# Splits of mixer B and of the memory queued behind the gates' evictions in a fused decoder layer

## The chip, the cores and the metric

The kernel runs on one core of a Trainium2 chip. The five engines of a core are named as the profile names them, and each has a queue of instructions of its own: TensorE (PE: matmuls), VectorE (DVE), ScalarE (ACT), GpSimd (POOL) and SyncE (SP, which issues the DMA transfers here). The metric is the device time of one execution in microseconds (us); the median of several executions is given.

## The reference

One layer of a decoder over 256 tokens of width 1024, in float32. Its core, with the helper functions left out:

```python
h = rmsnorm(x, norm_w[l])
proj = h @ w_in[l]                       # q, k, v of three dilation groups (mixer A), of mixer B, gates, ...
o_a = dilated_mixture(groups, slopes_a)  # 3 groups, 8 heads of 64, ALiBi, causal windows
o_b = moba_attention(heads(b_q), heads(b_k), heads(b_v), slopes_b)   # 8 heads, one block of 256 here
kv = rmsnorm(mem, mem_norm_w[l]) @ w_mem_kv[l]
o_m = memory_cross_attention(heads(m_q), heads(m_k), heads(m_v))     # 4 heads, 256 memory tokens
p_a = (o_a * jax.nn.silu(a_gate)) @ w_branch_a[l]
p_b = (o_b * jax.nn.silu(b_gate)) @ w_branch_b[l]
p_m = (o_m * jax.nn.silu(m_gate)) @ w_branch_m[l]
g_a, g_b, g_m = jnp.split(jax.nn.sigmoid(merge_logits + b_merge[l]), N_BRANCHES, axis=-1)
x = x + (g_a * p_a + g_b * p_b + g_m * p_m) @ w_out[l]
return rmsnorm(x, final_norm_w)
```

## The kernel before

All weights are cut into chunks of 128 x 2048 numbers (1 MB) that a list, PLAN, puts in order. Chunks 0 to 5 make mixer B's queries, keys and values (Bq, Bk, Bv), 6 and 7 the gate of mixer B, 8 and 9 the gate of mixer A, 10 the gate of the memory branch, 11 its query (Mq), 12 and 13 its keys and values (Mk, Mv), 14 and on mixer A, then the merge gates, the branch projections and the output projection. The loop over PLAN does for chunk i: start the load of chunk i + 3 on SP, split chunk i + 2, multiply, evict.

Splitting means that a float32 number is kept as two numbers of the type fp32r, which the matmuls take: ACT casts (`wh`, L93), DVE subtracts that from the number and keeps what is left (`wl`, L94). Each projection is then three matmuls per 128 rows: high by high and low by high (L232, L233, alternating), and at the end of a half chunk eight of high by low weights (L235). A chunk has two halves of 24 matmuls. There are three buffers for raw weights, three for `wh`, two for `wl`, so a load waits for the split of the chunk three before, and the split of the lower part of a chunk for PE's end of the chunk two before.

Outputs of a chunk lie in one of three PSUM banks (pool `pj`), so chunk i + 3 can begin only when chunk i is evicted. A gate is evicted by a tanh on ACT (`thg`, L645) and one instruction on DVE (`g`, L647) that reads the bank a second time.

Mixer B's queries and keys are split too, per half of the heads: `split_q` (two instructions on ACT, L271, two on DVE, L272) and `split_k` (four and four, L283 and L284, L289 and L290). The memory is scaled and split by eight instructions on ACT (`mh`, L218) and eight on DVE (`ml`, L219), and its mean squares by two on ACT (L171). In the loop these stand at chunks 6 to 11, in the middle of the projections that don't need them yet: the first to read Bq, Bk and the memory's parts is chunk 12.

The attention of mixer B runs in four pairs of heads (`pair_steps_b`): scores on PE (`sb`), a reduction and an exponential, a normalisation on DVE (`u`, L313 and L314), six transposes on PE (`pt`, L320), a copy on ACT, the product with the values (`ob`). Its steps are put into the loop at half chunks by a list of due times (`chain` and `pump`): the first pair's scores stand in the middle of chunk 12, its transposes in the middle of chunk 13, the second pair's transposes in chunk 14.

PE's order is that of the program from chunk 8 on. On the other engines a scheduler orders the instructions by its own estimate of when each is ready, unless `tc.issue_after` says that one is to stand behind another on its queue.

Of the kernel before, what the change touches and what calls it, by code (L numbers as in the profile page):

```python
# [1 line left out]

# [8 lines left out]
AF = mybir.ActivationFunctionType  # L11
ALU = mybir.AluOpType
# [51 lines left out]
def kernel(ctx: ExitStack, tc: tile.TileContext, wts: bass.AP, xT_d: bass.AP, memT_d: bass.AP,  # L64
                      x_d: bass.AP, mem_d: bass.AP, xr_d: bass.AP, fnw_d: bass.AP, con_d: bass.AP, out: bass.AP):
    nc = tc.nc
# [85 lines left out]
    for k in range(KD):  # L152
        nc.scalar.activation(xh[:, k, :], xT[:, k, :], AF.Copy, scale=nw[:, k:k + 1])
        nc.vector.scalar_tensor_tensor(xl[:, k, :], xT[:, k, :], nw[:, k:k + 1], xh[:, k, :].bitcast(F32),
                                       op0=ALU.mult, op1=ALU.subtract)
# [53 lines left out]
    def mem_norm():  # L209
        memst["r"], memst["dg"] = stats(memst["nat"], "m")  # L210
# [54 lines left out]
    def split_q(src, scale, name):  # L265

        xs = []
        for s in range(2):
            own, other = halves(s)
            t = rp.tile([P, 512], F32R, tag="r", name=f"{name}x{s}")  # L270
            nc.scalar.mul(t[own], src[own], scale)  # L271
            nc.vector.scalar_tensor_tensor(t[other], src[own], scale, t[own].bitcast(F32), op0=ALU.mult,  # L272
                                           op1=ALU.subtract)
            xs.append(t)
        return [t.rearrange("p (f t) -> p f t", f=2) for t in xs]

    def split_k(src, name):

        ys, zs = [], []
        for s in range(2):  # L280
            own, other = halves(s)
            t = rp.tile([P, 512], F32R, tag="r", name=f"{name}y{s}")
            nc.scalar.copy(t[own], src[own])  # L283
            nc.scalar.copy(t[other], src[own])  # L284
            ys.append(t)
        for s in range(2):
            own, other = halves(s)
            z = rp.tile([P, 512], F32R, tag="r", name=f"{name}z{s}")
            nc.vector.tensor_tensor(z[own], src[own], ys[s][own].bitcast(F32), op=ALU.subtract)  # L289
            nc.vector.tensor_tensor(z[other], src[own], ys[s][own].bitcast(F32), op=ALU.subtract)  # L290
            zs.append(z)
        return [t.rearrange("p (f t) -> p f t", f=2) for t in ys + zs]
# [6 lines left out]
    qkv, gate, og, steps, ths, acc = {}, {}, {}, [], {}, {}  # L299
# [224 lines left out]
                cs = slice(512 * (n // 2), 512 * (n // 2 + 1))  # L524
                nc.sync.dma_start(out[P * t:P * (t + 1), cs], yt[:, cs])

    late = []

    def evac_b(i, kind, key, ps, ps1):
        t = qkv[kind, key] = rtile(f"{kind}{key}")  # L530
# [15 lines left out]
    for i, (kind, key, src, col) in enumerate(PLAN):  # L546
# [15 lines left out]
        if i + 2 < NCH:  # L562
            for j in range(2 if i < 2 else 1):
                split(i + 2, j, 4 if i < 2 else 2)
        if i in (6, 8):
            hf = (i - 6) // 2
            qkv["Bqx", hf] = split_q(qkv["Bq", hf], 1.0, f"Bq{hf}")
        if i in (7, 11):
            hf = (i - 7) // 4
            qkv["Bkx", hf] = split_k(qkv["Bk", hf], f"Bk{hf}")  # L570
        if i == 9:
            mem_norm()
        if i in (10, 11):
            mem_split(4 * (i - 10), 4 * (i - 9))
        nat = kind[0] == "B"
        ah, al = (XH, XL) if nat else (HH, HL)
        if src == "mem":
# [4 lines left out]
        else:  # L582
            if i == 0:
                pss = [pa.tile([P, 512], F32, tag=("s", "pt")[f // 2], name=f"pj0{f}") for f in range(4)]
            elif i > 1:
                ps = pj.tile([P, 512], F32, tag="pj", name=f"pj{i}")
# [17 lines left out]
        if kind[0] == "B":  # L604
            late.append((i, kind, key) + ((pss[2 * i], pss[2 * i + 1]) if i < 2 else (ps, None)))
            if i >= 3:
                for z in [z for z in late if i == 5 or z[0] > 1]:
                    evac_b(*z)
                    late.remove(z)
                if i > 3:  # L610
                    split_h(4 * i - 16, 4 * i - 12)
                if i < 5:

                    with tc.issue_after(lower[i + 1].ins):
                        make_h(4 * i - 12, 4 * i - 8)
        elif kind in ("Aq", "Ak", "Av", "Mq", "Mk", "Mv"):
            at = (kind,) + (key if kind[0] == "A" else (0,))
            if kind[1] == "q" and at[-1] == 0:
                qkv[at] = split_q(ps, -SCALE, f"{kind}{i}")
            elif kind == "Mk":  # L620
                t = rtile("Mk")
                nc.vector.tensor_tensor(t.rearrange("p (f t) -> p f t", f=2), ps.rearrange("p (f t) -> p f t", f=2),
                                        rb["m"][:, None, :].to_broadcast([P, 2, S]), op=ALU.mult)
                qkv[at] = split_k(t, f"{kind}{i}")
            elif kind == "Mv":
                t = qkv[at] = rtile(f"{kind}{i}")
                for n in range(2):
                    nc.scalar.activation(t[:, S * n:S * (n + 1)], ps[:, S * n:S * (n + 1)], AF.Copy,
                                         scale=memst["r"][:, n:n + 1])
            elif kind[1] == "k" and at[-1] == 0:  # L630
                qkv[at] = split_k(ps, f"{kind}{i}")
            elif kind == "Av" and key[1] > 0:

                hf, g = key
                if g == 1:
                    stacked[hf] = tp.tile([P, 2, 2, S], F32, tag="vs", name=f"vs{hf}")
                for r in range(2):
                    nc.scalar.copy(stacked[hf][64 * (g - 1):64 * g, :, r, :],
                                   ps[64 * r:64 * (r + 1)].rearrange("p (e c) -> p e c", e=2))
            else:  # L640
                t = qkv[at] = rtile(f"{kind}{i}")
                nc.scalar.mul(t, ps, -SCALE if kind == "Aq" else 1.0)
        elif kind == "G":
            th = tp.tile([P, 512], F32, tag="th", name="thg")
            nc.scalar.activation(th, ps, AF.Tanh, scale=0.5)  # L645
            g = gate[key] = rp.tile([P, 512], F32, tag="g", name=f"g{i}", bufs=5)
            nc.vector.scalar_tensor_tensor(g, th, 1.0, ps, op0=ALU.add, op1=ALU.mult)  # L647
        elif kind == "L":
            br, bk = key
            th = ths[br, bk] = tp.tile([P, 512], F32, tag="th", name="thl")  # L650
            off = {"a": 0, "b": 8, "m": 16}[br]
            for n in range(2):
                c = off + 2 * bk + n
                nc.scalar.activation(th[:, S * n:S * (n + 1)], ps[:, S * n:S * (n + 1)], AF.Tanh, bias=hb[:, c:c + 1],
                                     scale=0.5)
        elif kind == "W":
            br, hf = key
            kn = 2 if br == "m" else 4
            oh = [og[br, k][0] for k in range(kn)]
            ol = [og[br, k][1] for k in range(kn)]  # L660
            if "t" not in acc:
                acc["t"] = cp.tile([P, 4, 512], F32, tag="xt", name="acc")
            for j in range(2):
                bk = 2 * hf + j
                ps = pj.tile([P, 512], F32, tag="pj", name=f"pw{i}{j}")
                for n in range(2):
                    mm_feat(ps, S * n, i, kn, 512, 2 * j + n, oh, ol)
                    if j == 1 and n == 0 and i + 2 < NCH:
                        split(i + 2, 1, 2)
                a = acc["t"][:, bk, :]  # L670
                if br == "b":
                    nc.vector.scalar_tensor_tensor(a, ths[br, bk], 1.0, ps, op0=ALU.add, op1=ALU.mult)
                else:
                    tmp = tp.tile([P, 512], F32, tag="mt", name="mt", bufs=1)
                    nc.vector.scalar_tensor_tensor(tmp, ths[br, bk], 1.0, ps, op0=ALU.add, op1=ALU.mult)
                    if br == "m":
                        nc.gpsimd.tensor_tensor(a, a, tmp, op=ALU.add)
                    else:
                        nc.vector.tensor_tensor(a, a, tmp, op=ALU.add)
                        mh = rp.tile([P, 2, S], F32R, tag="r", name=f"mgh{bk}")  # L680
                        ml = rp.tile([P, 2, S], F32R, tag="r", name=f"mgl{bk}")
                        nc.scalar.copy(mh.rearrange("p a b -> p (a b)"), a)
                        nc.vector.tensor_tensor(ml.rearrange("p a b -> p (a b)"), a,
                                                mh.rearrange("p a b -> p (a b)").bitcast(F32), op=ALU.subtract)
                        merged[bk] = (mh, ml)
                if j == 0:
                    pump(i, 0)
        else:
            if key < 2:
                order = [(key, i, 0), (key, i, 1)]  # L690
            elif key == 2:
                order = [(key, i, 0)]
            else:
                order = [(key, i, 0), (key - 1, i - 1, 1), (key, i, 1)]
            for kc, wi, t in order:
                out_mm(kc, wi, t)
                if t == 0 and i + 2 < NCH:
                    split(i + 2, 1, 2)
                if kc == 3:
                    finish(t)  # L700
# [74 lines left out]
```

## Time and profile before

| what | value |
|---|---|
| median of three runs | 353.12 us (352.27 to 354.44) |
| profiled execution | 352.46 us |
| its span, from the first instruction to the last | 350.6 us |
| mean granted TensorE clock | 0.989 |
| PE busy | 337.4 us (96%) |
| DVE busy | 232.5 us (66%) |
| ACT busy | 208.6 us (60%) |
| POOL busy | 28.3 us (8%) |
| chain that ended last, by engine | PE 84%, DVE 6%, DMA 5%, ACT 2% |
| data moved | 63.33 MB, mean 181 GB/s |

The page gives the busy times; the waits say which engine waited for which line and how long; the timeline lists the instructions of one engine in order of time, with equal neighbours merged; the stretches (windows) give each engine's busy time and the clock that the chip granted to PE between two moments. A clock of 1.00 is the higher of PE's two levels, 2.4 GHz, and 0.50 the lower, 1.2 GHz. Times within the execution count from the start of the span.

### The profile page before, as it was taken

What the parts mean: (1) busy time and instruction counts of PE and PEld (TensorE: products, weight loads), DVE (VectorE), ACT (ScalarE), POOL (GpSimd) and SP (SyncE); (2) the same over time, 40 slices, a digit from 0 to 9 for tenths busy, and PEclk for the clock granted to TensorE, in tenths of its full rate; (3) what the DMA queues carried; (4) which work ended last, traced back from release to release, by engine and by line L of the source; (5) the groups of instructions that cost most, each with busy time, mean ns of one, the idle gap of its engine ahead of it and who ended that gap; (6) DMA issues with size and microseconds to landing.
All of it is one profiled execution on the core that took longest, in us unless ns stands there. A gap on an engine that the chain in (4) does not pass through costs nothing.

```text
span 350.6 us, 7110 instructions
## 1 busy us (share of the span) xinstructions
PE 337.4 (96%) x2924; PEld 324.0 (92%) x2924; DVE 232.5 (66%) x402; ACT 208.6 (60%) x372; POOL 28.3 (8%) x40
## 2 busy tenths in 40 slices
PE   7999996999989999999999999999999999999992
PEld 4999995999989999899999999999999999999882
DVE  3859999658887457568756356866544748567554
ACT  6767899437776557766656365764643465546222
POOL 2501000000101000000101000010000214000022
PEclk9999998799999999999999999999999999999999
DMA  7997786646334463345333535444334366646003
GB/s 208 335 411 299 278 333 246 227 143 218 121 121 151 158 235 121 120 138 222 121 133 117 222 133 202 160 133 168 121 122 171 130 241 240 226 143 233 0 3 121
DMA packets 12945, 63.33 MB, mean 181 GB/s; under 512 B 1392, under 2 KB 2800, under 8 KB 6640
## 3 DMA queue, kind: packets, MB, share of 16 engines
q1 hardware_dynamic: 12912, 62.88, 49.9%
q8 instruction: 23, 0.38, 0.4%
q14 instruction: 10, 0.08, 0.1%
HBM read 61.82 MB, written 1.05 MB: 179 GB/s over the span
## 4 chain that ended last, share of the span: by engine, by line
PE 84%; DVE 6%; DMA 5%; ACT 2%; issue 1%; SPq 1%; POOL 0%; POOLq 0%; DVEq 0%
PE pj L232 16%; PE pj L235 16%; PE pj L233 16%; PE pj L252 4%; PE pj L254 4%; PE pj L253 4%; PE pt L320 3%; PE pw L232 3%; PE pw L233 3%; PE pw L235 3%; DMA wraw<-in_wts 3%; DMA xn<-in_x 2%; PE y L492 2%; PE y L491 2%; PE y L493 2%; DVE wl L94 2%
## 5 line engine op out<-in xcount | busy, mean ns | idle before, releaser
L94 DVE TENSOR_TENSOR wl<-wraw,wh 128x1024 fp32r<-128x1024 f32 (+2 forms) x117 | 129.4, 1143 | 60.1 <-issue 33.8
L93 ACT CAST wh<-wraw 128x1024 fp32r<-128x1024 f32 (+2 forms) x117 | 108.0, 968 | 49.9 <-PE pj L233 33.9
L232 PE MATMUL pj<-hh,wh 128*128 128x256 f32 x480 | 116.3, 284 | 3.4 <-DVE g L647 3.4
L233 PE MATMUL pj<-hl,wh 128*128 128x256 f32 x480 | 114.9, 280 | 0.2 <-DVE hl L199 0.2
L232 PEld LDWEIGHTS pj<-hh,wh 128*128 128x128 f32 x480 | 91.6, 191 | 4.5 <-issue 4.1
L233 PEld LDWEIGHTS pj<-hl,wh 128*128 128x128 f32 x480 | 91.6, 191 | 0.4 <-DVE hl L199 0.4
L235 PE MATMUL pj<-hh,wl 128*128 128x256 f32 x480 | 65.6, 280 | 0.0
L235 PEld LDWEIGHTS pj<-hh,wl 128*128 128x128 f32 x480 | 60.2, 190 | 0.0
L252 PE MATMUL pj<-wh,hh 128*128 128x256 f32 x96 | 26.9, 281 | 0.0
L254 PE MATMUL pj<-wh,hl 128*128 128x256 f32 x96 | 26.6, 277 | 0.0
L253 PE MATMUL pj<-wl,hh 128*128 128x256 f32 x96 | 26.6, 277 | 0.0
L321 ACT COPY ptsb<-pt 128x384 f32<-128x384 f32 (+1 forms) x28 | 13.2, 496 | 22.4 <-PE pt L320 22.4
L312 ACT ACTIVATE u<-u,st 128x384 f32<-128x384 f32 (+2 forms) x32 | 16.8, 527 | 10.2 <-DVE st L306 10.0
L252 PEld LDWEIGHTS pj<-wh,hh 128*128 128x128 f32 x96 | 18.0, 188 | 0.1
L253 PEld LDWEIGHTS pj<-wl,hh 128*128 128x128 f32 x96 | 18.0, 188 | 0.0
L254 PEld LDWEIGHTS pj<-wh,hl 128*128 128x128 f32 x96 | 18.0, 188 | 0.0
L314 DVE TENSOR_SCALAR u<-u,st 128x256 f32<-128x256 f32 (+2 forms) x40 | 15.5, 396 | 0.9
L354 POOL TENSOR_SCALAR nba<-con 128x512 f32<-128x512 f32 x8 | 5.0, 623 | 125.2 <-DVE st L306 124.8
L492 PE MATMUL y<-wl,mgh 128*128 128x512 f32 (+1 forms) x40 | 13.9, 348 | 0.0
L491 PE MATMUL y<-wh,mgh 128*128 128x512 f32 (+1 forms) x40 | 13.9, 347 | 0.0
L493 PE MATMUL y<-wh,mgl 128*128 128x512 f32 (+1 forms) x40 | 13.9, 346 | 0.0
L320 PE MATMUL pt<-con,u 128*128 128x128 f32 x88 | 12.5, 277 | 1.2 <-DVE u L314 1.2
(195 smaller groups left out, 549.2 us busy)
## 6 DMA issues: line engine op xcount, KB each, us to landing
wraw<-in_wts SPq DMA_DIRECT2D x48, 1024.0 KB, 4.8
wraw<-in_wts SPq DMA_DIRECT2D x15, 256.0 KB, 5.8
xn<-in_x SPq DMA_DIRECT2D x1, 1024.0 KB, 8.5
memT<-in_memT SPq DMA_DIRECT2D x1, 1024.0 KB, 5.6
memn<-in_mem SPq DMA_DIRECT2D x1, 1024.0 KB, 7.8
xres<-in_xr SPq DMA_DIRECT2D x1, 1024.0 KB, 6.0
wraw<-in_wts SPq DMA_DIRECT2D x2, 512.0 KB, 3.2
out<-ysb SPq DMA_DIRECT2D x4, 256.0 KB, 2.0
```

The costliest lines, as they stand in the source:

```text
L93: nc.scalar.copy(whs[i][:, sl], raws[i][:, sl])
L94: lower[i] = nc.vector.tensor_tensor(wls[i][:, sl], raws[i][:, sl], whs[i][:, sl].bitcast(F32), op=ALU.subtract)
L232: nc.tensor.matmul(ps[:, lo:lo + S], wh[:, k, fs], ah[k], start=(k == 0), stop=False)
L233: nc.tensor.matmul(ps[:, lo:lo + S], wh[:, k, fs], al[k], start=False, stop=False)
L235: nc.tensor.matmul(ps[:, lo:lo + S], wl[:, k, fs], ah[k], start=False, stop=(k == kn - 1))
L252: nc.tensor.matmul(ps[:, lo:lo + S], ah[k], wh[:, k, :], start=(k == 0), stop=False)
L253: nc.tensor.matmul(ps[:, lo:lo + S], ah[k], wl[:, k, :], start=False, stop=False)
L254: nc.tensor.matmul(ps[:, lo:lo + S], al[k], wh[:, k, :], start=False, stop=(k == KD - 1))
L320: nc.tensor.transpose(ps[:, P * j:P * (j + 1)], u[:, P * c:P * (c + 1)], ident)
L491: nc.tensor.matmul(y[t, n][:, 0:w], ht, wh[:, k, cs], start=(kc == 0 and k == 0), stop=False)
L492: nc.tensor.matmul(y[t, n][:, 0:w], ht, wl[:, k, cs], start=False, stop=False)
L493: nc.tensor.matmul(y[t, n][:, 0:w], lt, wh[:, k, cs], start=False, stop=(kc == 3 and k == 1))
```

## The change

The splits of mixer B and of the memory are taken from chunks 6 to 11, where they stood, to chunks 7, 9, 10 and 11, and each is told to stand behind both instructions of a gate's eviction on its queue: the first half's queries and keys behind gate 6, the memory behind gate 8, the second half's queries and keys behind gate 9. The instructions are the same ones.

```diff
--- before.py
+++ after.py
@@ -1,4 +1,4 @@
-from contextlib import ExitStack
+from contextlib import ExitStack, contextmanager
 
 import concourse.bass as bass
 import concourse.tile as tile
@@ -524,7 +524,14 @@
                 cs = slice(512 * (n // 2), 512 * (n // 2 + 1))
                 nc.sync.dma_start(out[P * t:P * (t + 1), cs], yt[:, cs])
 
-    late = []
+    late, gates = [], {}
+
+    @contextmanager
+    def behind_gate(i):
+
+        th, g = gates[i]
+        with tc.issue_after(th.ins), tc.issue_after(g.ins):
+            yield
 
     def evac_b(i, kind, key, ps, ps1):
         t = qkv[kind, key] = rtile(f"{kind}{key}")
@@ -562,16 +569,20 @@
         if i + 2 < NCH:
             for j in range(2 if i < 2 else 1):
                 split(i + 2, j, 4 if i < 2 else 2)
-        if i in (6, 8):
-            hf = (i - 6) // 2
-            qkv["Bqx", hf] = split_q(qkv["Bq", hf], 1.0, f"Bq{hf}")
-        if i in (7, 11):
-            hf = (i - 7) // 4
-            qkv["Bkx", hf] = split_k(qkv["Bk", hf], f"Bk{hf}")
-        if i == 9:
-            mem_norm()
-        if i in (10, 11):
-            mem_split(4 * (i - 10), 4 * (i - 9))
+        if i in (7, 10):
+            hf = (i - 7) // 3
+            with behind_gate(i - 1):
+                qkv["Bqx", hf] = split_q(qkv["Bq", hf], 1.0, f"Bq{hf}")
+                if i == 7:
+                    qkv["Bkx", hf] = split_k(qkv["Bk", hf], f"Bk{hf}")
+        if i == 11:
+            with behind_gate(9):
+                qkv["Bkx", 1] = split_k(qkv["Bk", 1], "Bk1")
+        if i in (9, 10):
+            with behind_gate(8):
+                if i == 9:
+                    mem_norm()
+                mem_split(4 * (i - 9), 4 * (i - 8))
         nat = kind[0] == "B"
         ah, al = (XH, XL) if nat else (HH, HL)
         if src == "mem":
@@ -642,9 +653,9 @@
                 nc.scalar.mul(t, ps, -SCALE if kind == "Aq" else 1.0)
         elif kind == "G":
             th = tp.tile([P, 512], F32, tag="th", name="thg")
-            nc.scalar.activation(th, ps, AF.Tanh, scale=0.5)
+            a = nc.scalar.activation(th, ps, AF.Tanh, scale=0.5)
             g = gate[key] = rp.tile([P, 512], F32, tag="g", name=f"g{i}", bufs=5)
-            nc.vector.scalar_tensor_tensor(g, th, 1.0, ps, op0=ALU.add, op1=ALU.mult)
+            gates[i] = (a, nc.vector.scalar_tensor_tensor(g, th, 1.0, ps, op0=ALU.add, op1=ALU.mult))
         elif kind == "L":
             br, bk = key
             th = ths[br, bk] = tp.tile([P, 512], F32, tag="th", name="thl")
```

What that does to the queues is seen in three places. The names carry the chunk's number: `wh9` is the upper part of chunk 9's weights, `thg` the tanh of a gate out of the bank `pj6` of chunk 6, `mh` and `ml` the memory's parts, `Bq0x` and `Bk0y`, `Bk0z` the parts of mixer B's first half, `Bq1x` and so on those of the second.

ACT ahead of the tanh of chunk 6, before:

```order
L218 ACTIVATE mh_857<-memT_505,small_174 128x256 x8
L93 CAST wh9_642<-wraw9_573 128x1024 x2
L271 ACTIVATE Bq1x0_721<-Bq1_565 64x512
L271 ACTIVATE Bq1x1_724<-Bq1_565 64x512
L283 CAST Bk1y0_928<-Bk1_429 64x512
L284 CAST Bk1y0_928<-Bk1_429 64x512
L645 ACTIVATE thg_636<-pj6_585 128x512
```

ACT around the same tanh, with the change:

```order
L93 CAST wh8_575<-wraw8_501 128x1024 x2
L93 CAST wh9_636<-wraw9_573 128x1024 x2
L656 ACTIVATE thg_630<-pj6_579 128x512
L271 ACTIVATE Bq0x0_640<-Bq0_562 64x512
L271 ACTIVATE Bq0x1_643<-Bq0_562 64x512
L283 CAST Bk0y0_646<-Bk0_427 64x512
```

The memory's casts and the second half's splits have left the place ahead of the tanh, and the first half's, which stood further ahead, now come behind it; chunk 9's weight casts are all that still stands between chunk 8's and the tanh.

DVE ahead of gate 6 (`g6`, which reads `thg` and the bank), before:

```order
L219 SCALAR_TENSOR_TENSOR ml_858<-memT_505,small_174,mh_857 128x256 x8
L94 TENSOR_TENSOR wl9_643<-wraw9_573,wh9_642 128x1024 x2
L272 SCALAR_TENSOR_TENSOR Bq1x0_721<-Bq1_565,Bq1x0_721 64x512
L272 SCALAR_TENSOR_TENSOR Bq1x1_724<-Bq1_565,Bq1x1_724 64x512
L289 TENSOR_TENSOR Bk1z0_934<-Bk1_429,Bk1y0_928 64x512
L290 TENSOR_TENSOR Bk1z0_934<-Bk1_429,Bk1y0_928 64x512
L647 SCALAR_TENSOR_TENSOR g6_638<-thg_636,pj6_585 128x512
```

DVE around the same gate, with the change:

```order
L94 TENSOR_TENSOR wl8_576<-wraw8_501,wh8_575 128x1024 x2
L658 SCALAR_TENSOR_TENSOR g6_632<-thg_630,pj6_579 128x512
L272 SCALAR_TENSOR_TENSOR Bq0x0_640<-Bq0_562,Bq0x0_640 64x512
L272 SCALAR_TENSOR_TENSOR Bq0x1_643<-Bq0_562,Bq0x1_643 64x512
L289 TENSOR_TENSOR Bk0z0_652<-Bk0_427,Bk0y0_646 64x512
L290 TENSOR_TENSOR Bk0z0_652<-Bk0_427,Bk0y0_646 64x512
L94 TENSOR_TENSOR wl9_637<-wraw9_573,wh9_636 128x1024
```

The gate now stands right behind chunk 8's split, and the lower parts of mixer B's first half are between it and chunk 9's.

DVE at the end of the softmax of mixer B's first pair (`u_1052` is the first head, `u_1065` the second; each has two pieces), before:

```order
L314 TENSOR_SCALAR u_1052<-u_1052,st_1053 128x256
L313 RECIPROCAL st_1066<-st_1066 128x1
L314 TENSOR_SCALAR u_1052<-u_1052,st_1058 128x128
L313 RECIPROCAL st_1071<-st_1071 128x1
L314 TENSOR_SCALAR u_1065<-u_1065,st_1066 128x256
L314 TENSOR_SCALAR u_1065<-u_1065,st_1071 128x128
L94 TENSOR_TENSOR wl14_1012<-wraw14_922,wh14_1011 128x1024 x2
L622 TENSOR_TENSOR Mk_1102<-pj12_1015,rb_m_975 128x512
```

The same place with the change:

```order
L314 TENSOR_SCALAR u_1052<-u_1052,st_1053 128x256
L314 TENSOR_SCALAR u_1052<-u_1052,st_1058 128x128
L313 RECIPROCAL st_1066<-st_1066 128x1
L94 TENSOR_TENSOR wl14_1012<-wraw14_930,wh14_1011 128x1024 x2
L633 TENSOR_TENSOR Mk_1102<-pj12_1015,rb_m_975 128x512
L313 RECIPROCAL st_1071<-st_1071 128x1
L314 TENSOR_SCALAR u_1065<-u_1065,st_1066 128x256
L314 TENSOR_SCALAR u_1065<-u_1065,st_1071 128x128
```

The second head's normalisation stood ahead of chunk 14's split and of the eviction of Mk, and now stands behind both.

PE's and POOL's orders are what they were. On SP the load of the residual (`xres`) has moved one place back, behind the load of chunk 13.

## Rows read from the trace of the kernel before

**Rows 1.** The page, busy time of each engine: us (share of the span) xinstructions.

```profile
PE 337.4 (96%) x2924; PEld 324.0 (92%) x2924; DVE 232.5 (66%) x402; ACT 208.6 (60%) x372; POOL 28.3 (8%) x40
```

**Rows 2.** The waits of PE: line waited for: us in total, times, longest.

```profile
PE pj L232 <- DVE g L647: 3.4, 1, 3.4
PE pt L320 <- DVE u L314: 1.2, 2, 1.0
```

**Rows 3.** Stretches: length, busy of PE, PEld, DVE, ACT, POOL, granted clock, DMA.

```profile
60.50:66.20 5.70, 5.69 (x27) 5.70 (x28) 5.29 (x9) 2.84 (x4) 0.71 (x1) 0.50 0.64 227
66.20:77.00 10.80, 10.80 (x96) 10.80 (x96) 5.64 (x6) 4.98 (x6) 0.00 (x0) 1.00 0.51 188
97.20:98.30 1.10, 0.10 (x3) 0.10 (x2) 1.10 (x7) 0.23 (x1) 0.00 (x0) 1.00 0.00 0
```

**Rows 4.** Timeline of PE: start us, us, what, idle before and releaser.

```profile
46.20 1.07 PE L235 MATMUL pj<-hh,wl 128*128 128x256 f32 x8
...
54.25 0.28 PE L232 MATMUL pj<-hh,wh 128*128 128x256 f32 x1
...
56.06 1.07 PE L235 MATMUL pj<-hh,wl 128*128 128x256 f32 x8
60.51 0.55 PE L232 MATMUL pj<-hh,wh 128*128 128x256 f32 x1 [3.38 <-DVE g L647]
...
66.18 0.28 PE L232 MATMUL pj<-hh,wh 128*128 128x256 f32 x1
```

**Rows 5.** Timeline of ACT, from the memory's casts to its squares.

```profile
46.80 3.31 ACT L218 ACTIVATE mh<-memT,small 128x256 fp32r<-128x256 f32 x8
50.01 1.99 ACT L93 CAST wh<-wraw 128x1024 fp32r<-128x1024 f32 x2
51.90 1.29 ACT L271 ACTIVATE Bq1x<-Bq 64x512 fp32r<-64x512 f32 x2
...
54.50 0.60 ACT L645 ACTIVATE thg<-pj 128x512 f32<-128x512 f32 x1
...
56.40 1.06 ACT L171 ACTIVATE memn<-memn 128x1024 f32<-128x1024 f32 x1
```

**Rows 6.** Timeline of DVE in the same stretch.

```profile
49.03 2.36 DVE L94 TENSOR_TENSOR wl<-wraw,wh 128x1024 fp32r<-128x1024 f32 x2
51.30 3.25 DVE L219 SCALAR_TENSOR_TENSOR ml<-memT,small,mh 128x256 fp32r<-128x256 f32 x8
54.47 2.36 DVE L94 TENSOR_TENSOR wl<-wraw,wh 128x1024 fp32r<-128x1024 f32 x2
56.86 1.39 DVE L272 SCALAR_TENSOR_TENSOR Bq1x<-Bq,Bq1x 64x512 fp32r<-64x512 f32 x2
58.26 0.68 DVE L289 TENSOR_TENSOR Bk1z<-Bk,Bk1y 64x512 fp32r<-64x512 f32 x1
...
59.67 0.69 DVE L647 SCALAR_TENSOR_TENSOR g<-thg,pj 128x512 f32<-128x512 f32 x1
```

**Rows 7.** Timeline of DVE, mixer B's first pair.

```profile
83.59 0.42 DVE L306 CUSTOM_DVE_ANT_0 u<-sb,nbb 128x256 f32<-128x256 f32 x1 [0.30 <-PE sb L297]
...
84.82 0.69 DVE L272 SCALAR_TENSOR_TENSOR Mq11x<-pj,Mq11x 64x512 fp32r<-64x512 f32 x1
...
86.79 2.36 DVE L94 TENSOR_TENSOR wl<-wraw,wh 128x1024 fp32r<-128x1024 f32 x2
89.18 0.69 DVE L622 TENSOR_TENSOR Mk<-pj,rb_m 128x512 f32<-128x512 f32 x1
```

**Rows 8.** Timeline of PE, transposes of mixer B's first and second pair.

```profile
89.13 0.82 PE L320 MATMUL pt<-con,u 128*128 128x128 f32 x6
89.71 0.36 PE L296 MATMUL sb<-Bk0y,Bq0x 128*128 128x256 f32 x1
...
98.23 0.98 PE L320 MATMUL pt<-con,u 128*128 128x128 f32 x6 [1.00 <-DVE u L314]
```

**Rows 9.** The page, DMA issues: KB each, median us from issue to landing.

```profile
wraw<-in_wts SPq DMA_DIRECT2D x48, 1024.0 KB, 4.8
```

## The prediction

> **What bounds the kernel now.** I read four views, in this order. First the busy times of the engines [rows 1]: TensorE (PE) is busy for 337.4 of the 350.6 us, VectorE (DVE) for 232.5, ScalarE (ACT) for 208.6. So the time is the sum of PE's work, and only a hole in PE's stream, or a slower clock under it, can be won. Second the waits of PE [rows 2]: one wait of 3.4 us, of the first matmul of a projection chunk for the line that makes a gate, and two waits of 1.2 us together, of the transposes of mixer B for normalised attention weights. Nothing else that the change can touch is on that list. Third the stretches around the long wait [rows 3]: from 60.5 to 66.2 us the granted clock is 0.50, the lower of its two levels (1.2 GHz); behind it it is 1.00 again; the small hole at 97.2 to 98.3 us left it at 1.00. Fourth the queues around that place [rows 4 to 8], to see why the gate was late and what the new order makes late in its place.
>
> Why the gate is late: projection outputs go to three PSUM banks in turn, so chunk 9 can't start before chunk 6's output is evicted. PE is done with chunk 6 at 47.27 us (46.20 + 1.07) and with chunk 8 at 57.13 [rows 4]. But ACT takes the tanh of chunk 6 at 54.50 only, behind the eight casts of the memory, chunk 9's weight casts and the splits for Bq1 and Bk1 [rows 5], and DVE makes gate 6 at 59.67, behind the matching lower parts [rows 6]. PE resumes at 60.51.
>
> **The change, part by part.** No instruction is added or removed on any queue; the order of PE and POOL stays as it was. ACT and DVE are reordered between chunk 6 and chunk 13, and on SP the load of the residual changes places with the load of chunk 13's weights. That residual is read only by the last lines of the kernel: cost nothing.
>
> Term 1, the wait. Sixteen matmuls take 1.81 us (54.25 to 56.06), so eight take 0.91, and without a wait chunk 9 would have begun at 56.06 + 0.91 = 56.97 instead of 60.51 [rows 4]: 3.54 us. Is gate 6 in time now? ACT has chunk 9's weight casts ahead of the tanh, and they wait for PE's end of chunk 6, 47.27, since they write its buffer. Two casts are 1.9 us from start to next start (50.01 to 51.90), the tanh 0.6 [rows 5]: 49.8 us; the gate on DVE 0.7 [rows 6]: 50.5. It is needed at 56.97. It is in time by 6 us, so the whole 3.54 is won.
>
> Term 2, the clock. From 60.51 to 66.18 there are 26 matmuls at the lower level (16 and 8 of the first half of the chunk, 2 of the second) [rows 3, 4], 5.67 us. At the upper level 24 matmuls take 2.72 us (54.25 to 56.97), 26 take 2.95. So 2.72 us more are won if PE doesn't stop. Terms 1 and 2: 6.26 us.
>
> Checks that nothing stops PE earlier. Chunk 9's lower weights: DVE does chunk 8's from 47.27 on (2.3 a pair [rows 6]), gate 6 to 50.5, two Bq0 parts to 51.9, two Bk0 parts, which wait for their casts on ACT (49.8 + 2.6 for four such casts, 51.90 to 54.50 [rows 5]: 52.4), to 53.8, the first half of chunk 9's, two Bk0 parts to 56.4, the second half: 57.6. PE wants them 16 matmuls into chunk 9, at 56.97 + 1.81 = 58.8. Margin 1.2, the smallest. Chunks 10, 11 and 12 come out at 60.6, 66.1 and 72.6 in the same way, wanted at 64.2, 69.7 and 75.6. Weights from DRAM: a load starts when the splits of the chunk three before are done and lands after 4.8 us [rows 9]; chunk 12's, the tightest, starts at 57.6, lands at 62.4, and ACT comes to it at 65.
>
> Term 3, the new wait. The splits that stood ahead of the gates now stand behind them, so DVE carries a backlog into mixer B's first attention pair. And there the order is new: before, all four normalisations stood ahead of chunk 14's split; now the second head's two stand behind that split and behind the evacuation of Mk. PE does the six transposes of that pair in two threes. When is the second head normalised? ACT: chunk 8 ends at 57.13, then chunk 11's casts 1.95, its tanh 0.6, two squares 2.1, the first memory cast 0.4 [rows 5]: 62.2 us. From there DVE is full: eight memory parts 3.17 (51.30 to 54.47), two small diagonals 0.4 (an estimate, half of one part each: they have 128 elements a row, the memory parts 256), four weight splits (chunks 11 to 14) at 2.32 (2.27 from 49.03 to 51.30, 2.39 from 54.47 to 56.86) 9.3, two gates 1.4, two Bq1 parts 1.4, four Bk1 parts 2.8 [rows 6], one Mq part 0.7, four score reductions 1.23 (83.59 to 84.82), the other Mq part and the small normalising instructions 1.97 (84.82 to 86.79), Mk 0.7 [rows 7]. Together 23.1: 85.3 us, and 0.13 more to PE. PE without a wait would begin these transposes at 89.13 - 6.26 = 82.87, the second three 0.3 later (six take 0.58) [rows 8]: 83.2. New wait: 85.4 - 83.2 = 2.2 us. Bounds: 1.5 if DVE's 23.1 are 3% shorter, 2.8 if one wait of 0.6 falls into them. The middle one is taken, as all its durations are rows of the same instructions.
>
> Term 4, the next pair. Its 1.00 us wait at 98.23 [rows 8] has the same cause (a DVE that is behind, with the normalisation after the split) in both orders. Taken as unchanged, with half a us to both sides. The third pair's last normalisation moves behind its split too, but in the last pair it already stood so, and all waits of these transposes outside the 1.00 are 0.2 us [rows 2]: nothing.
>
> Sum: 6.26 - 2.2 = 4.06 us. The profiled execution took 352.46 us (span 350.6 and 1.86 around it): 348.4. The median of the three runs, 353.12, lies 0.66 above it: **349.1 us**. From the bounds of terms 3 and 4: 347.9 to 350.2.
>
> **A rule about the clock.** The rows say: a hole of 3.4 us was followed by 0.50, one of 1.0 us by 1.00 [rows 3]. The new hole, 2.2 us, lies between, and no row shows one like it. The Trainium skill (TensorE: Matmul & The Clock Gate, section on HAM oscillation) says that each pause in the matmul stream that is long enough lets the gate throttle, and that the work behind the pause starts cold each time. By that rule the new hole could pay the price again, and could do so in some executions and not in others; by the sum it pays nothing. It is the second rival here.
>
> **The rivals.**
> 1. The new wait doesn't come: DVE catches up, 346.9 us (353.12 - 6.26). For it: DVE was busy for 5.64 of the 10.8 us from 66.2 on [rows 3]. Against it: that idle time is what the moved 7.4 us (memory 3.2, Bq1 1.4, Bk1 2.8) now fill. Chance 16%.
> 2. The new hole drops the clock. Price: that of term 2, 2.72 us, as the same number of matmuls would run at the lower level: 351.8. Against it: the hole at 97.2 us. Chance 18%.
> 3. Slower: the last normalisation behind the split stops PE in all four pairs of mixer B, each time for 2.2 us and each time with the clock falling (2.7): the first pair costs 2.7 over the sum, the other three 4.9 each, 17.4 in all: 366.5. It decides itself on whether DVE is still behind when the second pair begins; above a backlog of about 1 us it would repeat. Against it: the last pair has this order now and PE waits 0.2 us there at most. Chance 4%.
> 4. The change doesn't do what it says: PE stops at chunk 9 anyway, for the lower weights with their margin of 1.2 us, the clock falls, and the time stays: 353. Chance 5%.
> My forecast keeps 57%.
>
> **How the numbers follow.** A measurement of this kernel can tell about 1% from no change, 3.5 us: below 349.6 is faster, above 356.6 slower. The forecast lies only half a us on the faster side; some two thirds of its chance (0.39) are there, with rival 1 0.55. Within 1% are its rest (0.18), rivals 2 and 4: 0.41. Slower: 0.04. The range takes in the forecast's own (347.9 to 350.2), and reaches half a us beyond rival 1 at its lower end and beyond rival 2 at its upper, what one run's distance from the median may add: 346.4 to 352.3.
>
> **What the changed profile would show.** Terms 1 and 2: no wait of PE for the line of the gates, gate 6 made at about 50.5 us, chunk 9 beginning near 57.0 and the granted clock at 1.00 from 57 to 70 us. Term 3: a wait of PE's transposes for DVE's normalisation of 1.5 to 2.8 us near 83 us, with the split of chunk 14 ahead of it on DVE; a clock of 0.50 behind it is rival 2, no such wait rival 1. Term 4: a second wait of about 1 us some 11 us later. The forecast is wrong if PE stops at chunk 9 to 12 for weights, if the memory's split is late for chunk 12 (its last part comes at about 68, chunk 12 begins at 73.8), or if the third and fourth pair wait too.

## The result and the profile after

| | before | with the change |
|---|---|---|
| median of six runs each | 352.69 us (351.84 to 354.44) | 347.99 us (346.76 to 350.23) |
| ratio, 95% interval | | 0.9863 (0.9823 to 0.9903) |
| profiled execution, its span | 352.46, 350.6 us | 347.43, 345.6 us |
| span from the last lower-weight group of chunk 8 on | 294.54 us | 288.73 us |

The last row is 350.6 - 56.06 [rows 4] and 345.6 - 56.87 (below): it leaves out the first 57 us, in which the change touches none of PE's work or waits and in which executions differ by how soon the first weights arrive. From there on the profiled executions differ by 5.81 us, the medians by 4.7.

The busy times on the page, which answer to [rows 1], and the waits of PE, to [rows 2]:

```profile
PE 334.7 (97%) x2924; PEld 321.1 (93%) x2924; DVE 233.0 (67%) x402; ACT 208.8 (60%) x372; POOL 28.8 (8%) x40
```

```profile
PE pt L320 <- DVE u L314: 1.2, 2, 1.0
PE pwarm L137 <- DVE zero L108: 1.0, 1, 1.0
PE pj L232 <- ACT wh L93: 0.8, 1, 0.8
PE pj L245 <- ACT wh L93: 0.8, 1, 0.8
PE pj L233 <- DVE hl L199: 0.5, 1, 0.5
```

The wait for the gate's line is gone. The first row reads as before, 1.2 us in two pieces, but it is another wait now, as the timeline shows. The three waits for `wh` and `hl` lie ahead of 45 us.

PE's timeline (start us, us, what), to be read against [rows 4, 8]:

```profile
56.87 1.07 PE L235 MATMUL pj<-hh,wl 128*128 128x256 f32 x8
...
59.59 1.07 PE L235 MATMUL pj<-hh,wl 128*128 128x256 f32 x8
...
83.67 0.49 PE L320 MATMUL pt<-con,u 128*128 128x128 f32 x3
85.19 0.55 PE L320 MATMUL pt<-con,u 128*128 128x128 f32 x3 [1.03 <-DVE u L314]
...
93.05 0.89 PE L320 MATMUL pt<-con,u 128*128 128x128 f32 x6
```

Chunk 9's first lower-weight group starts 2.72 us after chunk 8's last, at full rate and without a hole. The six transposes of the first pair, one row before, are now two threes with 1.03 us of waiting between them, and the second pair's six have none.

The stretches (length, busy of PE, PEld, DVE, ACT, POOL, granted clock, DMA): the first is where PE waited before, the second answers to the slow stretch of [rows 3], the last begins at the end of the new hole:

```profile
57.00:60.50 3.50, 3.50 (x34) 3.50 (x32) 3.50 (x4) 3.43 (x5) 0.00 (x0) 1.00 0.37 105
60.50:66.20 5.70, 5.70 (x53) 5.70 (x52) 5.13 (x11) 5.70 (x14) 0.71 (x1) 1.00 0.99 384
...
85.20:90.00 4.80, 4.80 (x41) 4.80 (x42) 4.57 (x15) 3.90 (x12) 1.11 (x2) 1.00 0.51 207
```

The clock is 1.00 in all three, behind the new hole too.

ACT and DVE, against [rows 5 to 7]:

```profile
47.21 2.00 ACT L93 CAST wh<-wraw 128x1024 fp32r<-128x1024 f32 x2 [3.65 <-PE pj L233]
49.12 0.59 ACT L656 ACTIVATE thg<-pj 128x512 f32<-128x512 f32 x1
...
57.07 2.01 ACT L93 CAST wh<-wraw 128x1024 fp32r<-128x1024 f32 x2 [1.12 <-PE pj L233]
...
59.46 1.05 ACT L171 ACTIVATE memn<-memn 128x1024 f32<-128x1024 f32 x1
...
61.54 3.31 ACT L218 ACTIVATE mh<-memT,small 128x256 fp32r<-128x256 f32 x8
```

```profile
48.17 2.36 DVE L94 TENSOR_TENSOR wl<-wraw,wh 128x1024 fp32r<-128x1024 f32 x2 [2.57 <-issue]
50.45 0.68 DVE L658 SCALAR_TENSOR_TENSOR g<-thg,pj 128x512 f32<-128x512 f32 x1
...
62.08 0.89 DVE L219 SCALAR_TENSOR_TENSOR ml<-memT,small,mh 128x256 fp32r<-128x256 f32 x2 [0.23 <-ACT mh L218]
...
81.56 2.34 DVE L94 TENSOR_TENSOR wl<-wraw,wh 128x1024 fp32r<-128x1024 f32 x2
83.93 0.69 DVE L633 TENSOR_TENSOR Mk<-pj,rb_m 128x512 f32<-128x512 f32 x1
84.54 0.15 DVE L313 RECIPROCAL st<-st 128x1 f32<-128x1 f32 x1
84.61 0.53 DVE L314 TENSOR_SCALAR u<-u,st 128x256 f32<-128x256 f32 x2
85.31 0.68 DVE L289 TENSOR_TENSOR Mk12z<-Mk,Mk12y 64x512 fp32r<-64x512 f32 x1 [0.17 <-ACT Mk12y L283]
86.00 0.69 DVE L290 TENSOR_TENSOR Mk12z<-Mk,Mk12y 64x512 fp32r<-64x512 f32 x1
86.72 0.42 DVE L306 CUSTOM_DVE_ANT_0 u<-sb,nbb 128x256 f32<-128x256 f32 x1
```

The tanh of chunk 6 ends at 49.71 (before at 55.10) and gate 6 is made at 50.45 (before at 59.67). On DVE the second head's normalisation (84.61) stands behind chunk 14's split and Mk, as the order said. The last three rows are two of the lower parts of Mk and the second pair's first reduction.

### The profile page after: what moved, and what is told of

It is laid out like the page before. It is cut to its first block, busy times and chain, and to the rows that moved or that the text cites. A ratio compares the mean times of both kernels' runs of the same rounds, so it can differ in the third digit from the quotient of the medians.

```text
span 345.6 us, 7107 instructions
## 1 busy us (share of the span) xinstructions
PE 334.7 (97%) x2924; PEld 321.1 (93%) x2924; DVE 233.0 (67%) x402; ACT 208.8 (60%) x372; POOL 28.8 (8%) x40
## 4 chain that ended last, share of the span: by engine, by line
PE 80%; ACT 6%; DMA 5%; DVE 4%; issue 2%; SPq 1%; POOL 0%; POOLq 0%; DVEq 0%; ACTq 0%
PE pj L232 15%; PE pj L233 14%; PE pj L235 14%; PE pj L252 5%; PE pj L253 4%; PE pj L254 4%; PE pt L320 3%; PE pw L232 3%; PE pw L233 3%; PE pw L235 3%; DMA wraw<-in_wts 3%; DMA xn<-in_x 2%; PE y L491 2%; PE y L492 2%; PE y L493 2%; ACT wh L93 2%
## 5 line engine op out<-in xcount | busy, mean ns | idle before, releaser
L232 PE MATMUL pj<-hh,wh 128*128 128x256 f32 x480 | 114.5, 281 | 0.0
L233 PE MATMUL pj<-hl,wh 128*128 128x256 f32 x480 | 113.3, 278 | 0.5 <-DVE hl L199 0.5
L232 PEld LDWEIGHTS pj<-hh,wh 128*128 128x128 f32 x480 | 90.3, 188 | 1.0 <-issue 0.6
L233 PEld LDWEIGHTS pj<-hl,wh 128*128 128x128 f32 x480 | 90.4, 188 | 0.7 <-DVE hl L199 0.7
L235 PE MATMUL pj<-hh,wl 128*128 128x256 f32 x480 | 64.8, 278 | 0.0
L235 PEld LDWEIGHTS pj<-hh,wl 128*128 128x128 f32 x480 | 59.4, 188 | 0.0
L314 DVE TENSOR_SCALAR u<-u,st 128x256 f32<-128x256 f32 (+2 forms) x40 | 15.5, 396 | 0.9
```

Of the source, the lines that this page charges most:

```text
L232: nc.tensor.matmul(ps[:, lo:lo + S], wh[:, k, fs], ah[k], start=(k == 0), stop=False)
L233: nc.tensor.matmul(ps[:, lo:lo + S], wh[:, k, fs], al[k], start=False, stop=False)
L235: nc.tensor.matmul(ps[:, lo:lo + S], wl[:, k, fs], ah[k], start=False, stop=(k == kn - 1))
```

## The experiments

Theory: what the change wins is the hole before chunk 9 and the slow clock behind it; what it gives back is a wait of mixer B's transposes for a DVE that is behind. Rivals: one group of splits alone stood in the way; the places in the program make the gain, not the queues; the clock falls for another reason than the hole; the new order of the first pair, not DVE's backlog, makes the new wait. All ratios are to the kernel before on the same chip; E1 to E4 ran on one chip, E5, E6 and the two repeats on another. The edits are shown against the changed kernel, that of E4 against the kernel before.

**E1, the memory alone behind gate 8.**

```diff
-        if i in (7, 10):
-            hf = (i - 7) // 3
-            with behind_gate(i - 1):
-                qkv["Bqx", hf] = split_q(qkv["Bq", hf], 1.0, f"Bq{hf}")
-                if i == 7:
-                    qkv["Bkx", hf] = split_k(qkv["Bk", hf], f"Bk{hf}")
-        if i == 11:
-            with behind_gate(9):
-                qkv["Bkx", 1] = split_k(qkv["Bk", 1], "Bk1")
+        if i in (6, 8):
+            hf = (i - 6) // 2
+            qkv["Bqx", hf] = split_q(qkv["Bq", hf], 1.0, f"Bq{hf}")
+        if i in (7, 11):
+            hf = (i - 7) // 4
+            qkv["Bkx", hf] = split_k(qkv["Bk", hf], f"Bk{hf}")
```

> Only the memory's splits are queued behind gate 8; mixer B's four splits stay where they were before the change. Theory (what counts is when gate 6 is evicted, and whether the hole before chunk 9 is long enough to drop the clock): on VectorE the second half's six parts and chunk 9's split still stand ahead of gate 6, so it comes at about 57.8 + 0.7 = 58.5 us instead of 60.4, PE waits about 1.6 us instead of 3.4, the clock stays at 1.00, and the kernel gains 1.9 + 2.7 = 4.6 us (ratio 0.987), without a new wait in mixer B's first pair. Rival A (the memory alone stood in the way): the whole wait goes, 6.3 us (0.982). Rival B (mixer B's splits alone stood in the way): no gain, 1.00.

Measured: 349.58 us, ratio 0.9913 (0.9894 to 0.9931). PE's wait, at the start of chunk 9:

```profile
59.59 0.36 PE L232 MATMUL pj<-hh,wh 128*128 128x256 f32 x1 [1.59 <-DVE g L655]
```

1.59 us as worked out, the clock 1.00 behind it, no new wait at the first pair. Part of the gain, since the second half's splits still stand ahead of gate 6. The gain is 3.0 us where 4.6 were expected: the two executions profiled differ by 4.37 us from chunk 8 on (294.54 and 347.1 - 56.93 = 290.17), the medians by less; E4 shows the larger part of why.

**E2, mixer B alone behind gates 6 and 9.**

```diff
-        if i in (9, 10):
-            with behind_gate(8):
-                if i == 9:
-                    mem_norm()
-                mem_split(4 * (i - 9), 4 * (i - 8))
+        if i == 9:
+            mem_norm()
+        if i in (10, 11):
+            mem_split(4 * (i - 10), 4 * (i - 9))
```

> Only mixer B's four splits are queued behind gates 6 and 9; the memory's splits stay where the program had them, and on ScalarE and VectorE they now stand ahead of chunk 9's casts and chunk 8's lower part, where both engines stood idle in the changed kernel while they waited for chunk 6 to end. Theory: gate 6 at about 51 us, no hole, clock 1.00; VectorE has 3.2 us less to do behind the gates, so the first pair's transposes don't wait; the second pair waits 0 to 1 us. Gain 5.3 to 6.3 us, 0.982 to 0.985, somewhat more than the change. Rival A (the memory alone stood in the way): no gain, 1.00. Rival C (the backlog on VectorE doesn't matter, the new order of the first pair does): as much as the change, 0.986 to 0.987.

Measured: 347.14 us, 0.9845 (0.9828 to 0.9861). No hole, gate 6 at 51.38, no wait at the first pair, 1.00 us at the second. So moving mixer B's splits is enough, while moving the memory's alone leaves 1.59 us (E1). The memory's need not move: on ACT and DVE it fits into the time that both stood idle in the changed kernel until chunk 6 ended. At the first pair E2 also has the old order on DVE (normalisations ahead of chunk 14's split), so it doesn't tell DVE's backlog from the order there. DVE's row for gate 6:

```profile
51.38 0.71 DVE L657 SCALAR_TENSOR_TENSOR g<-thg,pj 128x512 f32<-128x512 f32 x1
```

**E3, the change's places in the program, without the rule.**

```diff
     def behind_gate(i):
-        th, g = gates[i]
-        with tc.issue_after(th.ins), tc.issue_after(g.ins):
-            yield
+        yield
```

> The splits stand at the change's places in the program, but without the rule that queues them behind the gates. The scheduler then puts the instructions in the same order on ScalarE and VectorE as before the change around gate 6. Theory: a wait of 3.4 us, the clock at 0.50 behind it, ratio 1.00. Rival (the places in the program, and with them the order of buffers and loads, make the gain): 0.987.

Measured: 352.59 us, 0.9992 (0.9974 to 1.001): no gain. The places do nothing, the queues do all. Its profiled execution (351.02 us) shows something that was not expected, the hole without the slow clock. PE's row at its end, and the stretches of the hole and behind it:

```profile
61.24 0.36 PE L232 MATMUL pj<-hh,wh 128*128 128x256 f32 x1 [2.83 <-DVE g L657]
```

```profile
58.30:61.24 2.94, 0.11 (x2) 0.03 (x1) 2.85 (x5) 2.94 (x5) 0.00 (x0) 1.00 0.83 284
61.24:66.20 4.96, 4.96 (x42) 4.96 (x43) 4.92 (x9) 2.79 (x4) 0.71 (x1) 1.00 0.64 258
```

**E4, the kernel before with work in the hole.**

```diff
+            if i == 9:
+                jk9 = pa.tile([P, 512], F32, tag="o", name="pjunk", bufs=1)
+                for _ in range(28):
+                    nc.tensor.matmul(jk9[:, 0:S], XH[0][:, 0:P], XH[0], start=True, stop=True)
```

> The kernel before the change, with 28 more matmuls of 128x256 (3.2 us at the upper clock) between chunks 8 and 9, whose result nobody reads: PE works in the hole instead of waiting. Theory (the hole drops the clock): the granted clock stays at 1.00, chunk 9 begins at the same 60.5 us, and the 2.7 us of the slow stretch come back: 350.0 us, ratio 0.992. Rival (the clock falls at this place for another reason, such as the load on the chip): 0.50 all the same, ratio 1.00. Rival (the extra matmuls cost their own time): 1.009.

Measured: 351.18 us, 0.9957 (0.9940 to 0.9973). PE in the hole, and the stretch that was slow:

```profile
57.96 3.52 PE L586 MATMUL pjunk<-xh 128*128 128x256 f32 x28
```

```profile
60.50:66.20 5.70, 5.70 (x51) 5.70 (x50) 5.46 (x12) 3.82 (x5) 0.57 (x1) 1.00 0.53 187
```

The clock stays at 1.00 and the kernel gains 1.4 us although it computes more. This one profile would not show that the hole drops the clock, since E3's kept 1.00 with the hole in it. The mean granted clock, which every run has, does: in the 17 runs of the kernel before on this chip it lies between 0.988 and 0.994, median 0.992, in E3's ten runs the median is 0.992 too, and in E4's five none is below 0.996.

But the gain is half of the 2.7 forecast, and it isn't a clean price of the clock. The edit did more than fill the hole: the scheduler also put the memory's lower parts behind gate 6 on DVE. Gate 6 on DVE and chunk 9's start on PE:

```profile
57.97 0.69 DVE L651 SCALAR_TENSOR_TENSOR g<-thg,pj 128x512 f32<-128x512 f32 x1
...
62.65 1.66 DVE L219 SCALAR_TENSOR_TENSOR ml<-memT,small,mh 128x256 fp32r<-128x256 f32 x4
```

```profile
61.31 0.28 PE L232 MATMUL pj<-hh,wh 128*128 128x256 f32 x1
```

Before, PE resumed 0.84 us after the gate's start [rows 4, 6]; by that it could have gone on here at about 58.8, and the extra matmuls held it until 61.31. They held it about as long as the wait had: chunk 9 starts 4.26 us after chunk 8's last lower-weight group (57.05), before 4.45. So the gain is still the clock's and not the wait's. Two estimates of the clock's usual price follow.

- From the time: 1.4 us were gained, but PE took 281.49 us from the start of chunk 9 to that of its last matmul (61.31 to 342.80), 0.5 more than in the profile before with its slow stretch put at the upper level (344.21 - 60.51 - 2.72 = 280.98). Together 1.9 us. The usual length of the wait isn't known (E3's, in the same order, was 0.55 us shorter than that of the profile before), so this is rough.
- From the mean clock: in E1, E2 and E4, 15 runs, it lies between 0.994 and 0.999, median 0.996. The difference to the kernel before, 0.004 of 350 us at half rate, is 2.8 us of slow clock, or 1.4 us of time. The mean also takes in slow clock while PE waits and behind PE's last matmul (0.50 from 342 to 344 us in the profile of the change), so this is rough too.

The execution profiled before paid 2.72: the price varies, and that one paid well above the usual 1.4 to 1.9.

**E5, the changed kernel with the first pair's normalisation ahead of chunk 14's split.**

```diff
+                    if i in (12,):
+                        with tc.issue_after(norms[-1].ins):
+                            split(i + 2, 0, 2)
+                            split(i + 2, 1, 2)
```

(`norms` collects the instructions of L314; the splits of that chunk at their old places are left out.)

> The changed kernel, with chunk 14's split told to stand behind the first pair's last normalisation on VectorE: the order that made the new wait is undone, and nothing else. Theory (VectorE's backlog decides, the order only which pair's transposes meet it): the 1.0 us wait at the first pair goes, and one of 0.7 to 1.5 us comes at the second pair; time as the changed kernel, within 0.4 us, ratio to before 0.985 to 0.988. Rival (the order alone made the wait): it goes and none comes, 1.0 us faster than the changed kernel, 0.983 to 0.984.

Measured: 348.32 us, 0.9889 (0.9855 to 0.9922). The transposes of the first and of the second pair:

```profile
84.05 0.82 PE L321 MATMUL pt<-con,u 128*128 128x128 f32 x6
...
92.72 0.52 PE L321 MATMUL pt<-con,u 128*128 128x128 f32 x3 [0.57 <-DVE u L315]
93.93 0.52 PE L321 MATMUL pt<-con,u 128*128 128x128 f32 x3 [0.69 <-DVE u L315]
```

The first pair's wait is gone, and 0.57 + 0.69 = 1.26 us have come at the second: the wait has moved. The edit moved more than the split, though. All four lower parts of Mk now stand ahead of the second pair's reductions (two did in the changed kernel):

```profile
87.53 0.69 DVE L290 TENSOR_TENSOR Mk12z<-Mk,Mk12y 64x512 fp32r<-64x512 f32 x1
88.25 0.42 DVE L307 CUSTOM_DVE_ANT_0 u<-sb,nbb 128x256 f32<-128x256 f32 x1
```

So that the wait moved is shown; that a backlog of DVE makes it move, and not this order, is argued. E6 sets the order of the second pair in a kernel whose DVE has the memory's 3.2 us less behind the gates.

**E6, E2 with the second pair's normalisation ahead of chunk 15's split.**

```diff
+                    if i in (13,):
+                        with tc.issue_after(norms[-1].ins):
+                            split(i + 2, 0, 2)
+                            split(i + 2, 1, 2)
```

> The kernel with mixer B's splits alone behind the gates (the memory's stay early), and in addition chunk 15's split told to stand behind the second pair's last normalisation on VectorE. There VectorE has no backlog at the first pair, and the wait of 1.0 us at the second pair stands behind that split of 2.3 us. Theory: the split is wanted some 6 us later only, so this wait goes, and no other comes but the 0.2 us one: 1.0 us faster than the kernel it is made from, about 346.2, ratio 0.981 to 0.983. Rival (the wait moves on to the third pair or to chunk 15's lower weights): as the kernel it is made from, 0.984 to 0.985.

Measured: 346.39 us, 0.9817 (0.9791 to 0.9843). The second pair's transposes, and DVE around that normalisation:

```profile
92.87 0.87 PE L321 MATMUL pt<-con,u 128*128 128x128 f32 x6
```

```profile
90.99 0.99 DVE L315 TENSOR_SCALAR u<-u,st 128x256 f32<-128x256 f32 x4
91.90 2.35 DVE L94 TENSOR_TENSOR wl<-wraw,wh 128x1024 fp32r<-128x1024 f32 x2
```

No wait: from chunk 8 on this profile has 345.2 - 58.04 = 287.16 us, 1.1 less than E2 (345.6 - 57.33 = 288.27). So the order alone removes the second pair's wait there, and it comes up nowhere else. This version is faster than the kernel before and, by 2.4 us on the same chip, than the changed kernel.

**The two repeats, E2 and the changed kernel beside E5 and E6.**

> The kernel with mixer B's splits alone behind the gates again, on the same chip as the two beside it: 347.1 us, ratio 0.983 to 0.986, one wait of 1.0 us at the second pair, none at the first.

Measured: 348.23 us, 0.9864 (0.9836 to 0.9892), the wait of 0.99 us at the second pair.

> The changed kernel again, on the same chip as the three beside it. By its profile its waits of PE add up to the same as those of the kernel with mixer B's splits alone behind the gates (1.0 us at the first pair instead of the second), so the theory expects the two within 0.4 us of each other: ratio 0.984 to 0.988. Rival (the hole at the first pair drops the clock in some executions): some runs 2 to 3 us longer than the others, with a mean granted clock of 0.989 to 0.991 instead of 0.994 to 0.999.

Measured: 348.79 us, 0.9893 (0.9863 to 0.9923). The intervals of the two overlap, as expected. Both came out a little above the ratios expected of them, and so did E5 (0.9889, at most 0.988 expected). From chunk 8 on the profiles have 344.8 - 56.49 = 288.31 and 348.5 - 59.71 = 288.79 us. The longest run, 350.28 us at 0.992, was the one profiled, and the first pair's hole is not what it paid for: its clock is 1.00 from 30 to 340 us. It had a hole of 1.89 us for weights at 25 us, and the clock fell behind that one:

```profile
23.20:25.16 1.96, 0.07 (x1) 0.00 (x1) 0.19 (x2) 1.96 (x6) 0.21 (x1) 1.00 1.01 409
25.16:27.00 1.84, 1.84 (x10) 1.84 (x11) 1.84 (x5) 1.51 (x3) 0.51 (x1) 0.67 1.05 430
27.00:29.00 2.00, 2.00 (x10) 1.82 (x9) 1.05 (x3) 0.42 (x2) 0.22 (x1) 0.50 0.49 201
29.00:31.00 2.00, 2.00 (x18) 2.00 (x18) 1.74 (x2) 1.84 (x2) 0.55 (x2) 0.95 0.90 295
```

So in the two executions of the change that were profiled the 1.0 us hole at the first pair dropped no clock; the run of 350.23 us at 0.989 in the result's six has no trace, and what it paid for stays open.

## Why the prediction was right

- **Term 1** (3.54 us): right. The wait for the gate is gone; gate 6 is made at 50.45 to 51.1, forecast 50.5. It stood behind chunk 8's split on DVE (the row at 48.17) and not, as the sum has it, behind the tanh, which had ended at 49.71. The margin of chunk 9's lower weights (56.65 + 1.23 = 57.9 on DVE; PE's group starts at 59.59) held.
- **Term 2** (2.72 us): the mechanism is right (E4), the size holds for the execution that it was read from, and is above the usual one, estimated at 1.4 to 1.9 us. A single profiled execution was taken for all.
- **Term 3** (-2.2 us): the wait came where forecast, behind chunk 14's split on a DVE without a pause to speak of, but with 1.03 us. DVE's sum was right: 23.06 us from the first memory part (62.08) to the end of the last normalisation (84.61 + 0.53), forecast 23.1. What failed is its start, "chunk 8 ends at 57.13, then chunk 11's casts". ACT's casts only overwrite the upper part of chunk 8's weights, which PE reads for the last time ahead of the eight lower-weight matmuls. The row at 57.07 says so: it ended a wait for PE L233, 0.87 us before the end of the group that started at 56.87. With that the sum gives 1.3. (Term 1 has the same step, "they wait for PE's end of chunk 6"; there it only made the margin look smaller.)
- **Term 4** (0): wrong. The second pair's wait of 1.00 us went, and of its cause as given, "a DVE that is behind, with the normalisation after the split", only the second half holds in the kernel before. DVE's rows there:

```profile
90.75 0.42 DVE L306 CUSTOM_DVE_ANT_0 u<-sb,nbb 128x256 f32<-128x256 f32 x1 [0.88 <-PE sb L297]
...
91.31 0.68 DVE L289 TENSOR_TENSOR Mk12z<-Mk,Mk12y 64x512 fp32r<-64x512 f32 x1
...
96.30 1.21 DVE L94 TENSOR_TENSOR wl<-wraw,wh 128x1024 fp32r<-128x1024 f32 x1
97.42 0.22 DVE L313 RECIPROCAL st<-st 128x1 f32<-128x1 f32 x2
97.55 0.99 DVE L314 TENSOR_SCALAR u<-u,st 128x256 f32<-128x256 f32 x4
```

DVE stood idle for 0.88 us until that pair's scores came; then four lower parts of Mk and chunk 15's split went ahead of the normalisations. It is the order that made this wait, and E6 removes it by order alone. In the changed kernel two of the four parts come ahead of the reductions (85.31, 86.00), and PE comes 1.03 us later by its new wait. Which of the two made the second pair's wait go isn't shown.

Together terms 3 and 4 gave back nothing: 1.03 us came and 1.00 went.

- **The sum**: with the terms as measured it is 3.54 + 2.72 - 1.03 + 1.00 = 6.23 us for the execution profiled before, where the two profiles differ by 5.81 from chunk 8 on. Of the 0.4 between, 0.3 lie behind PE's last matmul (338.91 to 345.6 with the change, 344.21 to 350.6 before). For a usual execution, with a wait as long, it is 4.9 to 5.4, less that 0.4; the medians differ by 4.7, and their interval allows 3.4 to 6.2. That the forecast of 4.06 came near is in part luck: a hole too large in term 3 and a wait not won in term 4 (2.2 us together) were partly made up by a clock too dear in term 2 (0.8 to 1.3 us). The measured 347.99 lies 1.1 below the forecast, inside its range, and 1.1 above rival 1; the time alone doesn't tell the two apart.
- **The rivals**: the new wait came (against 1, whose sum, nothing given back, is nevertheless what the waits add up to), no clock fell behind it in two profiles (against 2), the third and fourth pair wait no more than before (against 3), PE doesn't stop at chunk 9 (against 4).

## What to carry to other kernels

When an eviction is late, look at what stands ahead of it on its queues, and move only that: here mixer B's splits, not the memory's. A wait that an order takes away at one consumer can come up at the next (E5), so look at all of them. What won it here is to put work that is wanted late (a weight split) behind work that is wanted now (a normalisation), with less work queued ahead of both (E6). And read from the trace which instruction releases a buffer, the last that reads it, not the end of the stage.

## What the runs showed of the hardware

- The clock's price for a hole varies between executions and doesn't follow the hole's length alone: 3.38 us of waiting was followed by 5.7 us at 0.50 [rows 3], 2.83 us in E3's profile by 1.00, and 1.89 us at the start of the repeat of the change by 0.50 until about 29 us. The Trainium skill (TensorE: Matmul & The Clock Gate, section The HAM clock gate) says that the moment at which the chip judges the activity runs free of the kernel, so that one kernel differs from run to run; the three rows agree with that, but don't show that moment.
- Matmuls of 128x256 went at 0.113 us in most stretches and at 0.118 in others at the same granted clock of 1.00 (E4 behind the filled hole: 2.83 us for 24 instead of 2.72). The runs don't tell the cause.
